# First feed-forward of a decoder layer: from one pass over three token chunks to chunk 0 alone and then chunks 1 and 2 together

## Chip, cores and metric

The kernel runs on one core of a Trainium2 chip. The metric is the device time of one execution in microseconds (us); the kernel before took 2404.62 us, the median of three runs (2401.56 to 2405.68).

## What is computed

One decoder layer for 1024 prompt tokens and 8 sample tokens (1032 tokens of 1024 features): a half-step SwiGLU feed-forward, a mixer (sparse attention and retention), and a second half-step feed-forward, each with a residual and a layer norm. The change touches the first feed-forward and its layer norm.

```python
def swiglu(x, wg, wu, wd):
    return (jax.nn.silu(x @ wg) * (x @ wu)) @ wd

h = layer_norm(ALPHA * x + 0.5 * swiglu(x, ffn1_wg, ffn1_wu, ffn1_wd), ln1_g, ln1_b)
h = h @ w_in                        # split into the mixer's projections
...
h = layer_norm(ALPHA * h + 0.5 * swiglu(h, ffn2_wg, ffn2_wu, ffn2_wd), ln3_g, ln3_b)
```

`wg` and `wu` are 1024 x 2816, `wd` is 2816 x 1024, all float32.

## The kernel before

**Layout.** Activations lie transposed: features on the 128 partitions, tokens along the free axis, in three chunks of `CW` = 344 tokens (0, 1, 2), 8 blocks of 128 features each. A float32 product is made of three TensorE (PE) matmuls on rounded parts (`mm3`): high weight by high activation, high by low, low by high, at lines 169, 170 and 171. High parts are casts on ScalarE (ACT), low parts are differences on VectorE (DVE): `w_split` for weight tiles (L152, L154), L762 and L763 for the tokens. One dense tile of 128 output features for one chunk (`dense`) is thus 24 matmuls of 128x344.

**First feed-forward (class `Ffn`, tag `f1`).** The 2816 inner features are 22 tiles. Each has a gate tile `g`, an up tile `u` and a down tile `d` of 512 KB, loaded once on SyncE's (SP's) DMA queue (`w_raw`, L142) and used for all three chunks (`gateup_chunk`, `down`). The down products (L233 to L235) run by groups of two or four feature tiles and add into the residual `z` (L241).

**Start (`load_x`, `trunk`).** Nine blocks of up to 128 tokens are loaded (`xn`, L741), transposed on PE (`xt`, L754, two groups of four) and cast into the operands `xh` and `xl`. The first weights are split behind the first token blocks, and `z` is summed up on GpSimd (POOL, L768). `bias_rows` makes a table for the attention: a tiny matmul `bt` (L1278), a copy into the scratch tile `bra` in slot 20 (L1280), and a DMA that writes it 128 times over into DRAM (`scr`, L1281). That DMA is issued when all tokens and three feature tiles have been loaded.

**End.** After the last group's downs of a chunk its layer norm runs (`layer_norm`): `pm` (L645), a subtraction and squares on DVE and ACT, `pv` (L667), `pr` (L672), then the operands `h1h` and `h1l` (L682) of the next projections, `pw_ki` first. The norm of chunk 0 runs while PE makes the downs of chunks 1 and 2.

**Second feed-forward (class `Ffn2`, tag `f2`).** It is already split in two passes: `chunk0` makes chunk 0 with plain products, `chunks12` makes chunks 1 and 2 with gate and up by Strassen's seven products of half-size blocks (`ps0` to `ps6`) instead of eight; downs are plain in both. Its weights are loaded twice, by a class `Stream` that loads and splits tiles ahead as slots come free (L338 for whole tiles, L355 and L361 for sums and their split).

**Order.** The program's order on each engine is that in which the code issues; `Sched` interleaves the generators (`load_x`, `bias_rows`, layer norms) by modelled ticks, and on each engine instructions run in that order. Slots `A(g, slot, ...)` are numbered: a tile in a slot waits for whoever still uses the tile before it there.

Of the kernel before, what the change touches and what calls it, by code (L numbers as in the profile page):

```python
# [184 lines left out]
class Ffn:  # L185


    def __init__(self, g, wg, wu, wd, x, z, tag):
        self.g, self.wg, self.wu, self.wd, self.x, self.z, self.tag = g, wg, wu, wd, x, z, tag
        self.gt = {}  # L190
        self.groups = [[0, 1], *[list(range(f, f + 4)) for f in range(2, 22, 4)]]

    def weights(self, ft):
        g = self.g
        return (load_w(g, wcols(self.wg, ft * 128), f"{self.tag}g{ft}"), load_w(g, wcols(self.wu, ft * 128), f"{self.tag}u{ft}"))

    def gate_tile(self, ft):
        s = 14 + 2 * (ft % 5)
        self.gt[ft] = (A(self.g, s, f"gh_{self.tag}{ft}", F32R), A(self.g, s + 1, f"gl_{self.tag}{ft}", F32R))

    def gateup_chunk(self, ft, w, c):
        g, nc = self.g, self.g.nc
        x = self.x[c]
        th, tl = self.gt[ft]
        sl = slice(c * CW, (c + 1) * CW)
        pg = dense(g, w[0], x, f"pg_{self.tag}{ft}_{c}")
        s = g.ms.tile([P, CW], F32, tag="silu", name=f"s_{self.tag}{ft}_{c}", bufs=2)
        nc.scalar.activation(s, pg, AF.Silu)
        g.s.tick(0)
        pu = dense(g, w[1], x, f"pu_{self.tag}{ft}_{c}")  # L210
        nc.vector.tensor_tensor(out=s, in0=s, in1=pu, op=OP.mult)  # L211
        nc.scalar.copy(th[:, sl], s)
        nc.vector.tensor_tensor(out=tl[:, sl], in0=s, in1=th[:, sl].bitcast(F32), op=OP.subtract)
        g.s.tick(0)

    def gateup(self, ft):
        w = self.weights(ft)
        self.gate_tile(ft)
# [3 lines left out]
    def loaddown(self, grp):
        return [load_w(self.g, self.wd[ft * 128:(ft + 1) * 128, :].rearrange("p (k f) -> p k f", k=8), f"{self.tag}d{ft}") for ft in grp]

    def down(self, grp, ws, t0, t1, o):

        g = self.g
        sl = slice(t0, t1)
        p = bank(g, 'mm', f"pd_{self.tag}{grp[0]}_{t0}_{o}")
        for i, ft in enumerate(grp):  # L230
            th, tl = self.gt[ft]
            wh, wl = ws[i]
            g.nc.tensor.matmul(p[:, 0:t1 - t0], wh[:, o, :], th[:, sl], start=i == 0, stop=False)  # L233
            g.nc.tensor.matmul(p[:, 0:t1 - t0], wh[:, o, :], tl[:, sl], start=False, stop=False)  # L234
            g.nc.tensor.matmul(p[:, 0:t1 - t0], wl[:, o, :], th[:, sl], start=False, stop=i == len(grp) - 1)  # L235
        t = t0
        while t < t1:
            c = t // CW
            e = min(t1, (c + 1) * CW)
            z = self.z[c][:, o, t - c * CW:e - c * CW]  # L240
            g.nc.vector.scalar_tensor_tensor(out=z, in0=p[:, t - t0:e - t0], scalar=0.5 / ALPHA, in1=z, op0=OP.mult, op1=OP.add)  # L241
            t = e
        g.s.tick(0.44 * len(grp) * (t1 - t0) / CW)

    def middle(self):

        for gi, grp in enumerate(self.groups):
            for ft in grp:
                if ft not in self.gt:
                    self.gateup(ft)  # L250
            if gi + 1 < len(self.groups):
                if self.groups[gi + 1][0] not in self.gt:
                    self.gateup(self.groups[gi + 1][0])
                ws = self.loaddown(grp)
                for o in range(8):
                    for c in range(NCH):
                        self.down(grp, ws, c * CW, (c + 1) * CW, o)
# [2217 lines left out]
```

## Time and profile before

| what | us |
|---|---|
| median of three runs | 2404.62 |
| the profiled execution | 2399.24 |
| its span on the core | 2397.5 |
| PE busy in the span | 2284.9 (95%) |
| DVE busy | 1490.2 (62%) |
| ACT busy | 943.4 (39%) |
| GpSimd busy | 379.4 (16%) |
| first feed-forward's last matmul starts | 776.0 |

The span is that of the profiled execution, whose own time is 2399.24 us, 5.4 us under the median. PE's busy share is an average: what a stage is limited by is read from the windows and waits of that stage. "DMA share" in a window is the mean busy share of the core's 16 DMA engines.

### The profile page before, as it was taken

What the parts mean: (1) busy time and instruction counts of PE and PEld (TensorE: products, weight loads), DVE (VectorE), ACT (ScalarE), POOL (GpSimd) and SP (SyncE); (2) the same over time, 40 slices, a digit from 0 to 9 for tenths busy, and PEclk for the clock granted to TensorE, in tenths of its full rate; (3) what the DMA queues carried; (4) which work ended last, traced back from release to release, by engine and by line L of the source; (5) the groups of instructions that cost most, each with busy time, mean ns of one, the idle gap of its engine ahead of it and who ended that gap; (6) DMA issues with size and microseconds to landing.
All of it is one profiled execution on the core that took longest, in us unless ns stands there. A gap on an engine that the chain in (4) does not pass through costs nothing.

```text
span 2397.5 us, 36677 instructions
## 1 busy us (share of the span) xinstructions
PE 2284.9 (95%) x14495; PEld 2206.5 (92%) x14495; DVE 1490.2 (62%) x3262; ACT 943.4 (39%) x1722; POOL 379.4 (16%) x375
## 2 busy tenths in 40 slices
PE   8999999999999999898988999999999899999996
PEld 7999999999999998787767988899999899999995
DVE  5322323232226678678977667869756788787876
ACT  3121211212023555877445666436433443343331
POOL 3000000000003313454024225541000200000002
PEclk9999999999999999999989999989999999999998
DMA  6121211111021211222221215553544322222311
GB/s 160 36 79 36 62 45 53 40 49 53 18 71 58 88 33 46 56 75 56 66 72 33 55 46 180 178 161 99 157 132 138 117 77 71 88 72 65 94 54 48
DMA packets 211522, 186.93 MB, mean 78 GB/s; under 512 B 12074, under 2 KB 195190, under 8 KB 210582
## 3 DMA queue, kind: packets, MB, share of 16 engines
q1 hardware_dynamic: 206998, 171.93, 24.0%
q0 software_dynamic: 4352, 12.65, 1.9%
q8 instruction: 114, 1.87, 0.3%
q14 instruction: 58, 0.48, 0.1%
HBM read 163.39 MB, written 21.17 MB: 77 GB/s over the span
## 4 chain that ended last, share of the span: by engine, by line
PE 79%; DVE 10%; ACT 6%; issue 3%; DMA 1%; POOL 1%; POOLq 0%; SPq 0%; ACTq 0%; DVEq 0%
PE pu_f L169 5%; PE pg_f L171 5%; PE pu_f L171 5%; PE pu_f L170 5%; PE pg_f L169 4%; PE pg_f L170 4%; PE pd_f L233 3%; PE pd_f L235 3%; PE pd_f L234 3%; PE pds_f L467 2%; PE pds_f L468 2%; PE pds_f L469 2%; ACT ja L1019 2%; PE ps_f2U L169 2%; PE ps_f2U L170 2%
## 5 line engine op out<-in xcount | busy, mean ns | idle before, releaser
L211 DVE TENSOR_TENSOR s_f<-s_f,pu_f 128x344 f32<-128x344 f32 x66 | 33.8, 512 | 233.0 <-PE pu_f L171 233.0
L171 PE MATMUL pg_f<-xh,wl_f1g 128*128 128x344 f32 x528 | 169.6, 321 | 1.1 <-DVE wl_f1g L154 1.1
L169 PE MATMUL pg_f<-xh,wh_f1g 128*128 128x344 f32 x528 | 169.8, 322 | 0.0
L170 PE MATMUL pg_f<-xl,wh_f1g 128*128 128x344 f32 x528 | 169.1, 320 | 0.5 <-DVE xl L763 0.5
L233 PE MATMUL pd_f<-gh_f,wh_f1d 128*128 128x344 f32 x528 | 169.5, 321 | 0.0
L235 PE MATMUL pd_f<-gh_f,wl_f1d 128*128 128x344 f32 x528 | 169.2, 320 | 0.0
L169 PE MATMUL pu_f<-xh,wh_f1u 128*128 128x344 f32 x528 | 168.8, 320 | 0.0
L234 PE MATMUL pd_f<-gl_f,wh_f1d 128*128 128x344 f32 x528 | 168.8, 320 | 0.0
L170 PE MATMUL pu_f<-xl,wh_f1u 128*128 128x344 f32 x528 | 168.6, 319 | 0.0
L171 PE MATMUL pu_f<-xh,wl_f1u 128*128 128x344 f32 x528 | 168.5, 319 | 0.0
L241 DVE SCALAR_TENSOR_TENSOR z<-pd_f,z 128x344 f32<-128x344 f32 x144 | 73.9, 516 | 142.7 <-PE pd_f L235 142.5
L471 DVE SCALAR_TENSOR_TENSOR z<-pds_f,z 128x344 f32<-128x344 f32 x160 | 82.4, 516 | 73.3 <-PE pds_f L469 73.3
L606 POOL TENSOR_TENSOR lns_l<-z 128x344 f32<-128x344 f32 x4 | 5.4, 1348 | 711.1 <-DVE z L241 694.8
L716 POOL TENSOR_TENSOR yt<-yt,lot 128x512 f32<-128x512 f32 (+1 forms) x7 | 7.2, 1041 | 693.8 <-DVE lot L709 692.1
L467 PE MATMUL pds_f<-gs_f,wh_f2ds 128*128 128x344 f32 x352 | 113.0, 321 | 0.0
L468 PE MATMUL pds_f<-gs_f,wh_f2ds 128*128 128x344 f32 x352 | 112.7, 320 | 0.0
L469 PE MATMUL pds_f<-gs_f,wl_f2ds 128*128 128x344 f32 x352 | 112.5, 320 | 0.0
L1019 ACT ACTIVATE ja<-key,zt 128x1024 bf16<-128x1024 int16 (+5 forms) x90 | 93.8, 1043 | 42.9 <-DVE zt L1030 35.1
L152 ACT CAST wh_f1g<-wr_f1g 128x1024 fp32r<-128x1024 f32 x22 | 23.1, 1049 | 221.0 <-PE pd_f L234 170.4
L171 PEld LDWEIGHTS pg_f<-xh,wl_f1g 128*128 128x128 f32 x528 | 99.8, 189 | 1.4 <-DVE wl_f1g L154 1.4
L170 PEld LDWEIGHTS pg_f<-xl,wh_f1g 128*128 128x128 f32 x528 | 99.8, 189 | 0.8 <-DVE xl L763 0.8
L169 PEld LDWEIGHTS pg_f<-xh,wh_f1g 128*128 128x128 f32 x528 | 99.8, 189 | 0.2
(718 smaller groups left out, 7602.1 us busy)
## 6 DMA issues: line engine op xcount, KB each, us to landing
wr_f1g<-in_ffn_wg_dram SPq DMA_DIRECT2D x22, 512.0 KB
wr_f1u<-in_ffn_wu_dram SPq DMA_DIRECT2D x22, 512.0 KB
wr_f1d<-in_ffn_wd_dram SPq DMA_DIRECT2D x22, 512.0 KB
wr_f2u<-in_ffn_wu_dram SPq DMA_DIRECT2D x22, 512.0 KB
wr_f2g<-in_ffn_wg_dram SPq DMA_DIRECT2D x22, 512.0 KB
wr_f2dp<-in_ffn_wd_dram SPq DMA_DIRECT2D x22, 512.0 KB
wr_f2G<-in_ffn_wg_dram SPq DMA_DIRECT2D x22, 512.0 KB
wr_f2U<-in_ffn_wu_dram SPq DMA_DIRECT2D x22, 512.0 KB
```

Source lines behind the costliest of these rows:

```text
L169: g.nc.tensor.matmul(ps, w[0][:, k, :], x[0][:, k, :], start=first and i == 0, stop=False)
L170: g.nc.tensor.matmul(ps, w[0][:, k, :], x[1][:, k, :], start=False, stop=False)
L171: g.nc.tensor.matmul(ps, w[1][:, k, :], x[0][:, k, :], start=False, stop=last and i == n - 1)
L233: g.nc.tensor.matmul(p[:, 0:t1 - t0], wh[:, o, :], th[:, sl], start=i == 0, stop=False)
L234: g.nc.tensor.matmul(p[:, 0:t1 - t0], wh[:, o, :], tl[:, sl], start=False, stop=False)
L235: g.nc.tensor.matmul(p[:, 0:t1 - t0], wl[:, o, :], th[:, sl], start=False, stop=i == len(grp) - 1)
L241: g.nc.vector.scalar_tensor_tensor(out=z, in0=p[:, t - t0:e - t0], scalar=0.5 / ALPHA, in1=z, op0=OP.mult, op1=OP.add)
L467: g.nc.tensor.matmul(ps, wh[:, o, :], th, start=i == 0, stop=False)
L468: g.nc.tensor.matmul(ps, wh[:, o, :], tl, start=False, stop=False)
L469: g.nc.tensor.matmul(ps, wl[:, o, :], th, start=False, stop=i == len(grp) - 1)
L471: g.nc.vector.scalar_tensor_tensor(out=z, in0=ps, scalar=0.5 / ALPHA, in1=z, op0=OP.mult, op1=OP.add)
L1019: nc.scalar.activation(jk[:, 0:n], key[b], AF.Sign, bias=t[:, j:j + 1], scale=-1.0, accum_out=cnt[:, j:j + 1])
```

## The change

The first feed-forward is now made by `Ffn2` as well, and the class `Ffn` goes. Its first pass makes chunk 0 with plain products, and each finished block of `z[0]` is written to DRAM (`parked`). The second pass makes chunks 1 and 2 with the seven products for gate and up; the slots of chunk 0 hold the operands that this needs (`T1` to `T4`, by `load_x` and `lefts`). `z[0]` is then read back (`z10p`), and the layer norm of chunk 0 runs during the last downs of chunks 1 and 2 (`last`). All 66 weight tiles are loaded twice. `load_x` brings the tokens in at a slower pace, and copies `z` on ACT (L733 after). The number of PE matmuls of 128x344 in the first feed-forward goes from 4752 to 4488: each of the 11 pairs of feature tiles takes, for gate and again for up, 7 products of 12 matmuls in place of 8.

```diff
-class Ffn:
...
-            for c in range(NCH):
-                self.gateup_chunk(ft, w, c)
...
+    def end(self):
+        for p in (9, 10):
+            self.drop('s', self.pairs[p])
+            self.g.fs.put(*self.gt.pop(p)[1])
...
+def lefts(g, B, a, b, slots, free):
...
+    V.tensor_tensor(out=d3, in0=b[:, 4:8, :], in1=b[:, 0:4, :], op=OP.subtract)
+    V.tensor_tensor(out=d2, in0=d3, in1=a[:, 0:4, :], op=OP.add)
+    yield 1.0
+    split4(g, B, 'T2', slots[0], d2)
+    yield 2.0
+    split4(g, B, 'T3', slots[1], d3)
+    V.tensor_tensor(out=d2, in0=a[:, 4:8, :], in1=d2, op=OP.subtract)
+    while not free():
+        yield 0.25
+    split4(g, B, 'T4', slots[2], d2)
...
 def load_x(g, xp, xs, x, B, z):
...
+                nc.scalar.copy(z[c][:, ks, sl], src)
                 t = e
+        if b + 3 < 9:
+            fetch(b + 3)
         g.s.t += 0.6
-        if b in (2, 5, 8):
-            c = b // 3
-            nc.gpsimd.tensor_tensor(out=z[c], in0=x[c][0].bitcast(F32), in1=x[c][1].bitcast(F32), op=OP.add)
         g.xb = b + 1
-        yield 0 if b < 2 else 2.0
+        yield 0 if b < 2 else 10.0
...
     s.tick(0)
-    r0 = [w_raw(g, wcols(w, 0), n) for w, n in ((f1.wg, "f1g0"), (f1.wu, "f1u0"))]
+    f1.st.nraw = 2
+    f1.st.fetch()
     s.until(lambda: g.xb >= 3)
-    w0 = [tuple(w_split(g, r) for r in r0)]
+    f1.st.ahead(2)
...
     br = s.add(bias_rows(g, i['rel_bias'], i['oh'], g.scr), 6.0)
...
+        while s.live(br):
+            yield 1.0
+        g.fs.put(20, 21)
...
+    def parked(o):
+        psum['ls'].add(o)
+        nc.sync.dma_start(zscr[0][:, o * CW:(o + 1) * CW], z[0][:, o, :])
...
+    f1.chunk0(x[0], hook, parked)
+    psum['out'] = True
+    setbanks(g, ch=[0, 1, 2, 3], dn=[4, 5], aux=[6, 7])
+    f1.chunks12(B, ready)
...
+    z[0] = X8(g, "z0", "z10p")
+    for q in range(2):
+        nc.sync.dma_start(z[0][:, 4 * q:4 * q + 4, :].rearrange("p k t -> p (k t)"), zscr[0][:, 4 * q * CW:(4 * q + 4) * CW])
...
+    lns[0] = s.add(ln1(0, psum['ls']), 4.0)
...
+    for c in (1, 2):
         ls = LnSum(g, z[c], f"l1{c}")
...
+        f1.last(c, after)
...
         lns[c] = s.add(ln1(c, ls))
+    f1.end()
```

**The start, on ACT.** The first casts of the program, before and after. `xt0_0` to `xt2_1` are the transposed token blocks 0 to 2, whose casts the first product of chunk 0 needs; `wr_f1g0` is the loaded gate tile 0, `wh_` its high part.

Before:

```order
L762 CAST xh0_91<-xt0_0_112 128x4x128
L762 CAST xh0_91<-xt0_1_119 128x4x128
L762 CAST xh0_91<-xt1_0_128 128x4x128
L762 CAST xh0_91<-xt1_1_135 128x4x128
L152 CAST wh_f1g0_163<-wr_f1g0_106 128x1024
L762 CAST xh0_91<-xt2_0_144 128x4x88
L762 CAST xh0_91<-xt2_1_153 128x4x88
```

After:

```order
L273 CAST wh_f1g0_169<-wr_f1g0_0_105 128x1024
L731 CAST xh0_91<-xt0_0_109 128x4x128
L731 CAST xh0_91<-xt0_1_117 128x4x128
L273 CAST wh_f1u0_175<-wr_f1u0_0_107 128x1024
L273 CAST wh_f1g1_206<-wr_f1g1_0_173 128x1024
L733 COPY z10_95<-xt0_0_109 128x4x128
L733 COPY z10_95<-xt0_1_117 128x4x128
L273 CAST wh_f1u1_238<-wr_f1u1_0_179 128x1024
L731 CAST xh0_91<-xt1_0_127 128x4x128
L731 CAST xh0_91<-xt1_1_135 128x4x128
```

Four weight casts and the copies of `z` now stand between the casts of the token blocks.

**The store of the table, on SP's queue.** `scr` is the table's write, `wr_f1g3`, `wr_f1u4`, `wr_f1dp2` are weight tiles, `xn7` a token block.

Before:

```order
L142 DMA wr_f1d0_808<-in_ffn1_wd_dram 128x1024
L142 DMA wr_f1d1_814<-in_ffn1_wd_dram 128x1024
L1281 DMA scr_60<-bra_253 1024x1x384
L142 DMA wr_f1g3_1012<-in_ffn1_wg_dram 128x8x128
L142 DMA wr_f1u3_1018<-in_ffn1_wu_dram 128x8x128
```

After:

```order
L710 DMA xn6_311<-in_x_prompt_dram 128x1024
L1254 DMA scr_60<-bra_256 1024x1x384
L710 DMA xn7_418<-in_x_prompt_dram 128x1024
L228 DMA wr_f1u4_0_424<-in_ffn1_wu_dram 128x8x128
L228 DMA wr_f1dp2_0_461<-in_ffn1_wd_dram 128x1024
L228 DMA wr_f1dp3_0_483<-in_ffn1_wd_dram 128x1024
L228 DMA wr_f1g5_0_505<-in_ffn1_wg_dram 128x8x128
L228 DMA wr_f1u5_0_527<-in_ffn1_wu_dram 128x8x128
```

The store now stands among the loads of the first pass. The tile `wl_f1u3` (low part of up tile 3) is made in slot 20, where `bra` lay, so that its split on DVE waits for the store to have landed; the load `wr_f1u5` in turn waits for the buffer that this split reads. On PE the first user of `wl_f1u3` stands here after:

```order
L171 MATMUL pg_f14_621<-xh0_91,wl_f1g4_502 128x344
L721 MATMUL xt6_0_666<-ident_65,xn6_311 128x128 x4
L721 MATMUL xt6_1_672<-ident_65,xn6_311 128x128 x4
L171 MATMUL pu_f13_585<-xh0_91,wl_f1u3_480 128x344
L169 MATMUL pu_f13_585<-xh0_91,wh_f1u3_479 128x344
```

There are 158 matmuls of 128x344 and three transposed blocks on PE between `bt` and that `pu_f13` matmul. Before, the next tile in slot 20 is `gh_f13`, which is written only after nine products of `gateup_chunk` (48 matmuls each).

**The end, on PE.** `pds_f118_2_4` is the fifth of eight down products of chunk 2, `pv_l11` a step of the layer norm of chunk 1, `pw_ki_0` the first projection, of chunk 0.

Before:

```order
L234 MATMUL pd_f118_688_7_6317<-gl_f121_5687,wh_f1d21_5873 128x344
L235 MATMUL pd_f118_688_7_6317<-gh_f121_5686,wl_f1d21_5875 128x344
L169 MATMUL pw_ki_0_6344<-h1h0_6128,wh_ki_5956 128x344
L170 MATMUL pw_ki_0_6344<-h1l0_6129,wh_ki_5956 128x344
L171 MATMUL pw_ki_0_6344<-h1h0_6128,wl_ki_5958 128x344
```

After:

```order
L405 MATMUL pds_f118_2_4_7270<-gs1_f120_6894,wl_f1ds21_6829 128x344
L635 MATMUL pv_l11_7308<-ones_70,lns_l11_7018 128x1 x3
L169 MATMUL pw_ki_0_7379<-h1h0_7180,wh_ki_7108 128x344
L169 MATMUL pw_qi0_0_7430<-h1h0_7180,wh_qi0_7142 128x344
L169 MATMUL pw_kr0_0_7466<-h1h0_7180,wh_kr0_7462 128x344
L170 MATMUL pw_ki_0_7379<-h1l0_7181,wh_ki_7108 128x344
L171 MATMUL pw_ki_0_7379<-h1h0_7180,wl_ki_7110 128x344
L169 MATMUL pw_ki_0_7379<-h1h0_7180,wh_ki_7108 128x344
L170 MATMUL pw_ki_0_7379<-h1l0_7181,wh_ki_7108 128x344
L403 MATMUL pds_f118_2_5_7291<-gs0_f118_6606,wh_f1ds18_6772 128x344
```

Seven projection matmuls on chunk 0's normalised operands now stand ahead of 36 downs of chunk 2. Between `pm_l10` and `pw_ki_0` there were 168 downs and there are 132; between `pm_l11` and `pv_l11` there were 101 matmuls of 128x344 and there are 36. From `pw_qi0_1` on, PE's order is the same in both.

## Rows read from the trace of the kernel before

**Rows 1.** Page: busy us, share, instructions; costliest group: busy, mean ns, idle before.

```profile
PE 2284.9 (95%) x14495; PEld 2206.5 (92%) x14495; DVE 1490.2 (62%) x3262; ACT 943.4 (39%) x1722; POOL 379.4 (16%) x375
L169 PE MATMUL pg_f<-xh,wh_f1g 128*128 128x344 f32 x528 | 169.8, 322 | 0.0
```

**Rows 2.** 50-us windows: length, busy (count) per engine PE PEld DVE ACT POOL, clock, DMA.

```profile
0.00:50.00 50.00, 41.01 (x239) 36.70 (x240) 32.43 (x38) 21.45 (x38) 19.86 (x9) 1.00 0.64 182
200.00:250.00 50.00, 50.00 (x318) 50.00 (x318) 15.19 (x27) 3.31 (x5) 0.00 (x0) 1.00 0.08 22
1700.00:1750.00 50.00, 50.00 (x320) 49.81 (x319) 30.91 (x41) 16.62 (x22) 0.00 (x0) 1.00 0.47 142
1900.00:1950.00 50.00, 40.73 (x236) 40.20 (x235) 49.37 (x91) 28.21 (x48) 14.70 (x9) 0.90 0.31 102
2000.00:2050.00 50.00, 50.00 (x319) 50.00 (x319) 39.91 (x74) 18.03 (x32) 0.00 (x0) 1.00 0.24 74
```

**Rows 3.** Timeline, PE, 0 to 22 us: start, length, instruction [idle before].

```profile
11.07 0.66 PE L169 MATMUL pg_f<-xh,wh_f1g 128*128 128x344 f32 x1
15.86 0.45 PE L171 MATMUL pg_f<-xh,wl_f1g 128*128 128x344 f32 x1
20.13 1.07 PE L754 MATMUL xt<-ident,xn 128*128 128x128 f32 x8 [1.92 <-issue]
```

**Rows 4.** Timeline, SP's queue, first 130 us.

```profile
11.35 0.32 SPq L1274 DMA_DIRECT2D bra<-in_rel_bias_dram  x1
12.65 0.32 SPq L1275 DMA_DIRECT2D bra<-in_oh_dram  x1
36.38 0.81 SPq L1281 DMA_DIRECT2D scr<-bra  x1
75.69 0.38 SPq L142 DMA_DIRECT2D wr_f1g<-in_ffn_wg_dram  x1
```

**Rows 5.** Costs of single instructions: timeline and line groups, ACT and DVE.

```profile
5.53 0.59 ACT L762 CAST xh<-xt 128x512 fp32r<-128x512 f32 x1 [3.53 <-PE xt L754]
L152 ACT CAST wh_f1g<-wr_f1g 128x1024 fp32r<-128x1024 f32 x22 | 23.1, 1049 | 221.0 <-PE pd_f L234 170.4
L154 DVE TENSOR_TENSOR wl_f1g<-wr_f1g,wh_f1g 128x1024 fp32r<-128x1024 f32 x16 | 19.6, 1226 | 40.1 <-ACT wh_f1g L152 40.1
```

**Rows 6.** DMA issues of the first 130 us: transfer, count, KB each.

```profile
scr<-bra SPq DMA_DIRECT2D x1, 1536.0 KB
```

**Rows 7.** 5-us windows around the end of that transfer, columns as in Rows 2.

```profile
65.00:70.00 5.00, 5.00 (x33) 5.00 (x33) 0.19 (x1) 0.46 (x1) 0.00 (x0) 1.00 0.43 48
70.00:75.00 5.00, 5.00 (x34) 5.00 (x33) 1.40 (x3) 1.89 (x3) 0.00 (x0) 1.00 0.02 5
```

**Rows 8.** Waits of PE, first 130 us: total, times, longest.

```profile
PE pg_f L171 <- DVE wl_f1g L154: 1.1, 1, 1.1
```

**Rows 9.** Waits of PE, 1868 to 1960 us.

```profile
PE ps_f2U L169 <- DVE pc_f2G L533: 5.5, 1, 5.5
PE ps_f2G L169 <- DVE lot L628: 3.8, 1, 3.8
```

**Rows 10.** 10-us window after those waits, columns as in Rows 2.

```profile
1920.00:1930.00 10.00, 10.00 (x52) 10.00 (x53) 9.85 (x16) 7.09 (x11) 0.48 (x1) 0.79 0.43 134
```

**Rows 11.** Timeline, DVE, in the same stretch.

```profile
1896.19 3.68 DVE L705 BATCH_NORM_STATS2 lot<-yp 128x6 f32<-128x512 f32 x6
```

**Rows 12.** Timelines, PE and DVE, first layer norm of chunk 0.

```profile
746.79 0.74 PE L645 MATMUL pm_l<-lns_l,ones 128*128 128x344 f32 x2
757.00 0.80 PE L667 MATMUL pv_l<-ones,lns_l 128*128 128x1 f32 x6
772.27 1.59 DVE L682 TENSOR_TENSOR h1l<-z,h1h 128x1376 fp32r<-128x1376 f32 x1
776.16 0.32 PE L169 MATMUL pw_ki<-h1h,wh_ki 128*128 128x344 f32 x1
```

**Rows 13.** Waits of PE, 700 to 850 us.

```profile
PE pv_l L667 <- DVE lns_l L657: 2.8, 2, 2.0
```

More of the change, by code (lines that the diff above doesn't have):

```diff
@@ L182, in dense @@
     return ps
-class Ffn:
[L188 to L218, printed above, removed]
-        for c in range(NCH):
-            self.gateup_chunk(ft, w, c)
[L222 to L257, printed above, removed]
@@ L264, in __init__, with get, take @@
         self.ids = list(ids)
+        self.first = ()
     def __len__(self):
         return len(self.ids)
-    def get(self):
-        return self.ids.pop(0)
+    def get(self, long=False):
+        q = next((q for q in self.ids if long and q in self.first), self.ids[0])
+        self.ids.remove(q)
+        return q
     def put(self, *ids):
         self.ids += ids
+    def take(self, ids):
+        self.ids = [q for q in self.ids if q not in ids]
 class Stream:
@@ L324, in want, with want_all @@
         return self.made[key]
+    def want_all(self):
+        while self.steps:
+            assert self.step(), "no room"
     def done(self, key):
@@ L504, in gates @@
         g = self.g
-        sl = [g.fs.get() for _ in range(3)]
+        sl = [g.fs.get(True) for _ in range(3)]
         t = [A(g, q, f"gs{j}_{self.tag}{f}", F32R, 3 * CW) for j, q in enumerate(sl)]
@@ L594, in last, with halves_of, split4 @@
             self.down('s', grp, c, {f: tiles[(f, c)] for f in grp}, o, after)
+def halves_of(t):
+    return t[:, 0:4, :], t[:, 4:8, :]
+def split4(g, B, nm, slot, src):
+    B[nm] = halves_of(X8(g, slot, f"op{nm}", F32R))
+    g.nc.scalar.copy(B[nm][0], src)
+    g.nc.vector.tensor_tensor(out=B[nm][1], in0=src, in1=B[nm][0].bitcast(F32), op=OP.subtract)
+def lefts(g, B, a, b, slots, free):
+    V = g.nc.vector
+    d3, d2 = (g.ms.tile([P, 4, CW], F32, tag="lnq", name=f"d{j}", bufs=2) for j in (3, 2))
+    V.tensor_tensor(out=d3, in0=b[:, 4:8, :], in1=b[:, 0:4, :], op=OP.subtract)
[8 more added lines that the diff above has]
+    split4(g, B, 'T4', slots[2], d2)
 class LnSum:
@@ L1988, in ln1, with after @@
         return layer_norm(g, z[c], ls.s, ln['ln1_g'], ln['ln1_b'], out, f"l1{c}", done)
[L1990 to L1999 removed]
+    lns[0] = s.add(ln1(0, psum['ls']), 4.0)
+    f1.st.want_all()
+    own = [q for q in g.fs.ids if q in ok][:6]
+    g.fs.take(own)
+    g.raws, g.ri, g.pairs, g.pi = own[0:2], 0, [tuple(own[2:4]), tuple(own[4:6])], 0
+    g.lo_eng = [nc.vector]
+    for nm in ('ki', 'qi0'):
+        rX[nm] = w_raw(g, wcols(w_in, colX[nm]), nm)
+    for c in (1, 2):
+        ls = LnSum(g, z[c], f"l1{c}")
+        def after(o):
+            ls.add(o)
+            if c == 1 and o in (4, 6):
+                nm = ('ki', 'qi0')[(o - 4) // 2]
                 wX[nm] = w_split(g, rX[nm])
+        f1.last(c, after)
         if c == 1:
@@ L2004, in trunk @@
         lns[c] = s.add(ln1(c, ls))
+    f1.end()
+    s.drain(lns[0])
+    g.fs.put(psum['slot'])
+    more = [q for q in g.fs.ids if q in ok][:6]
+    g.pairs += [tuple(more[j:j + 2]) for j in (0, 2, 4)]
     kst, kl = A(g, 18, "kst", F32R), A(g, 19, "kl", F32R)
```

104 lines of the change are left out of this document (43 added, 61 removed).

## Prediction

> **What bounds the kernel now.** I read the page first: PE is busy 95% of the span, and the costliest groups are the first feed-forward's matmuls, with next to no idle time ahead of them [rows 1]. So the time goes with the number of matmuls, except where PE waits. The 50-us windows say what one matmul costs: 318 to 320 in 50 us at full clock, 0.157 us each (the mean of 322 ns in rows 1 overlaps its neighbours and is not a rate). That holds in the first feed-forward, where DVE is busy 15.2 of 50 us, in the plain first pass of the second, at DVE 30.9 and 142 GB/s, and in its seven-product pass, at DVE 39.9 [rows 2]. So both passes that the first feed-forward is to get already run on this chip with PE full. What is left are the joints: the start, the change from one pass to the next, and the layer norm at the end. The reader should look there for PE below 50 in 50: 41.0 at the start, 40.7 at the joint of the second feed-forward [rows 2].
>
> **Term 1, the products.** 4752 matmuls become 4488: 264 x 0.157 = -41.4 us. Every extra DVE and ACT step of the seven products (+518 and +220 instructions) lies beside full PE, as in rows 2; if that cover were gone, the slower rival below gives the price. Twice the weights is cheap as long as a tile comes in time: in the plain pass three 512 KB tiles serve 72 matmuls, 11.3 us, which is 139 GB/s, what the window of 142 GB/s already shows; the peak needed is below the 182 GB/s of the first window [rows 2].
>
> **Term 2, the start.** Before, the stream begins at 11.07, at 0.29 us a matmul (half clock) until 15.86 [rows 3]. After, ACT casts four weight tiles and copies z between the casts of the token blocks, so it waits in order for loads. Loads land one after another: bra's first part is issued when one landing frees it and its second part at the next, 11.35 and 12.65, so 1.3 us per 512 KB [rows 4]. Gate tile 0 is the fourth load and lands near 8.8, up 0 10.1, gate 1 11.3, up 1 (a token block is ahead of it) 13.9, gate 2 15.2. With 1.05 us per weight cast and 0.59 per token cast or copy [rows 5]: cast of gate 0 to 9.85, two token casts 11.0, up 0 12.1, gate 1 13.1, two copies 14.3, up 1 15.3, two casts 16.5, two copies 17.7, gate 2 18.8, two short casts 19.8, then DVE's low parts: the full stream from about 21.2. About 13 matmuls at half clock cost 1.7 more, six later token blocks 0.8 each but for the last (20.13 to the next matmul [rows 3]), together 4.2, and bt 0.7: PE has lost 27.9 us in all. Before, 164 matmuls of 128x344 have begun by 50 us, a loss of 50 - 164 x 0.157 = 24.3 (the window counts 239 with some 75 transposes and small ones [rows 2]). So +3.6; bounds 0 (the casts find everything landed and PE starts as before) and 7.
>
> **Term 3, the table's store.** Before, it is issued at 36.38, when nothing is left to load until 75.69 [rows 4]. It moves 1536 KB [rows 6] at 48 GB/s with 0.43 of the engines' time, and ends about 70.5: the 65 to 70 window is still at 0.43, the next at 0.02 [rows 7]. That is 34.1 us, which nobody waits for. After, the split of up tile 3 on DVE stands behind it through slot 20. bt comes 83 matmuls and one token block after the stream's start: 21.2 + 13.0 + 1.7 + 0.8 = 36.8, the store is issued at 37.6 and lands at 71.8, the split (1.23 [rows 5]) ends at 73.1. PE gets to the matmul that needs it after bt (0.7), 158 matmuls (24.8) and three token blocks (2.4), at 64.7. It waits 8.4 us, with everything behind it in its order; DVE's next splits (up 4, the downs) and SP's load of up 5 are queued behind the same split, but up 4 is needed 22 matmuls later only. The half clock after a wait like this: a window after one holds 52 matmuls in place of 64 [rows 10], 12 x 0.157 = 1.9. Together +10.3; bounds 0 (the store is quick beside the loads, or goes early enough) and 16.
>
> The store could also begin later than it is issued: four loads of 512 KB stand ahead of it on the queue, and loads land one after another [rows 4], so up to 4 x 1.3 = 5.2 us more if none of them has run. The Trainium skill, page "DMA: Bandwidth & Descriptors", section "Queues, rings and completion order", says that each DMA engine consumes its ring's descriptors in order. By that page the store waits for whatever of the four is still queued, and the time would be up to 2388; the landings in rows 4 agree with such an order, but no row shows a load behind the store.
>
> **Term 4, a wait that goes.** PE's wait for the low part of a gate tile at 115 us, 1.1 us [rows 8], belongs to the old order of loads: -1.3 with the restart.
>
> **Term 5, from pass 1 to pass 2.** The second feed-forward pays 5.5 + 3.8 us there [rows 9] and 1.9 for the clock [rows 10], 11.2 in all, because DVE has the splits for the seven products and the output layer norm at once (49.4 of 50 busy [rows 2], six statistics of 3.68 us being the norm's first part [rows 11]). The first feed-forward has the splits, the downs' sums and T2 to T4 there, but no layer norm on DVE: its sums go to POOL. Counting the instructions from the last group's first down to the third product chain by their durations I get 51.5 us of DVE work beside 54.7 us of PE work. It just fits. I take +1, near the lower end, since the row of 11.2 holds work that is missing here; bounds 0 and 11.2.
>
> **Term 6, the end.** Before, from pm of chunk 0 to its operands (h1l done at 773.9) takes 27.1 us, and from pm to pv 10.2 us [rows 12]; 168 downs cover the first, 26.4 us, and PE waits 2.8 in all [rows 13]. After, 132 downs (20.7 us) are left ahead of the first projection, and 36 matmuls (5.7 us) between pm and pv of chunk 1, in place of 101. PE would wait 10.2 - 5.7 = 4.5 for pv, some 2 more for the operands (27.1 - 20.7 - 4.5), and 2 to 3 for pr of chunk 1 and the norm of chunk 2, which now follow close on each other: about 9, against 2.8. I take +6; bounds 0 and 10. The reload of z[0] (1.4 MB, by the 1.3 us per 512 KB of rows 4 under 4 us) lies under 96 downs of chunk 1 (15 us) and costs nothing; without that cover it would cost its 4 us once.
>
> The sums that POOL no longer makes and the slower pace of the token blocks lie beside full PE: nothing. From the second projection group of chunk 1 on PE's order is unchanged, so nothing more is to come.
>
> **Sum.** -41.4 + 3.6 + 10.3 - 1.3 + 1 + 6 = -21.8 us. From the profiled execution, 2399.2 us (span 2397.5 and 1.7 around it), that gives 2377.4. The median of the runs shown is 5.4 higher; the comparison is with it, so **2383 us**.
>
> **Rivals.** (A) The store costs nothing: 2383 - 10 = 2373. For it: the stall rests on one slot and on a margin of 8 us in 65, and the store may run faster when it starts in a stretch with other traffic. Against it: its 34 us were measured with the queue free. (B) The joint between the passes costs what it costs in the second feed-forward: 2383 + 10 = 2393. For it: the code is the same class and 51.5 against 54.7 leaves little, with waits inside that chain not counted. Against it: without the norm. (C) Slower: the stream of weights in pass 1 does not run ahead. Each of 66 tiles takes 1.3 + 1.05 + 1.23 = 3.6 us from the queue's turn to the split, and one tile lasts PE 3.8 us; as slots are also held by token blocks and the table until some 100 us in, tiles could come late by a part of this. From 0.4 us a tile on, 26 us, the gain is gone; at 0.6, 40 us, the time is 2423. Against it: the same pass in the second feed-forward has PE at 50.00 [rows 2]. (D) The change does not do what it says, the number of matmuls staying: excluded by the order, which has 264 fewer of 128x344, and none elsewhere changed.
>
> **Chances.** Forecast, 2377 to 2389: 0.53. A: 0.17. B, or the store's later start (at most 2388): 0.18. Both and a worse end, 2398 to 2409: 0.08. C: 0.04, D: 0. The range for 8 in 10 goes from 2367 (A with a better start) to 2398 (B with the end's upper bound). A measurement here can tell about 0.2%, 4.8 us: faster means under 2399.8 and gets 0.88, the same 0.08, slower 0.04.
>
> **What will show it.** The number of 128x344 matmuls and 50.00 of 50 in the windows from 100 to 400 and in the pass after (term 1, C). The first full product near 21 us on PE (term 2). One wait of PE on the low part of up tile 3 near 65 us, about 8 us long, that ends 1.2 us after the table's store has landed (term 3, A). PE's waits between 270 and 310 us, where the passes meet, on sums or splits of DVE: 0 to 2 us, or 9 (term 5, B). PE's waits on pv, h1h, h1l and pr before the mixer, 9 in all (term 6). The forecast is wrong above all if PE has gaps spread over pass 1, or if the joints do not stand where I put them.

## The result, and the profile after

The changed kernel takes **2379.3 us** (median of five runs, 2376.15 to 2386.46); the kernel before, run beside it, 2401.6. The ratio is 0.9914 with a 95% interval of 0.9889 to 0.9940, so 22 us less. The forecast was 2383; of the 4 us between them 3 are the kernel before itself, which took 2404.6 when the forecast was made and 2401.6 in this run. The profiled execution went from 2399.24 to 2376.15 us, 23.1 less; the sum ahead of the result had 21.8.

The page and the 50-us windows of the changed kernel, columns as in [rows 1] and [rows 2]:

```profile
PE 2245.4 (95%) x14231; PEld 2165.0 (91%) x14231; DVE 1773.3 (75%) x3780; ACT 1077.2 (45%) x1942; POOL 361.8 (15%) x372
```

```profile
0.00:50.00 50.00, 35.34 (x200) 32.83 (x201) 21.41 (x32) 27.58 (x45) 0.69 (x6) 1.00 0.70 202
50.00:100.00 50.00, 41.97 (x258) 41.51 (x257) 25.61 (x38) 18.76 (x30) 0.00 (x0) 0.90 0.72 186
100.00:150.00 50.00, 50.00 (x323) 49.62 (x322) 34.96 (x46) 20.91 (x30) 0.00 (x0) 1.00 0.48 142
200.00:250.00 50.00, 50.00 (x319) 49.72 (x318) 29.53 (x43) 15.57 (x21) 0.00 (x0) 1.00 0.47 142
300.00:350.00 50.00, 49.52 (x314) 48.98 (x313) 44.28 (x82) 19.66 (x36) 0.00 (x0) 1.00 0.31 91
400.00:450.00 50.00, 50.00 (x319) 49.91 (x318) 41.42 (x78) 18.91 (x34) 0.00 (x0) 1.00 0.25 75
750.00:800.00 50.00, 49.08 (x298) 47.49 (x298) 38.65 (x61) 27.35 (x47) 15.04 (x12) 0.95 0.32 118
```

PE is busy 39.5 us less and DVE 283 us more, still beside it. From 100 to 300 and from 350 to 700 us PE is full, 318 to 323 matmuls in 50 us, as in [rows 2]; the plain pass moves 142 GB/s, the pass with the seven products has DVE at 38 to 44. What is not full is the start, the stretch from 50 to 100 and the end of the feed-forward near 750. The timeline of PE at the start and at the table's store, that of SP's queue for the store, and that of DVE:

```profile
4.57 1.94 PE L721 MATMUL xt<-ident,xn 128*128 128x128 f32 x8 [4.57 <-DMA xn<-in_x_prompt_dram]
13.42 1.97 PE L721 MATMUL xt<-ident,xn 128*128 128x128 f32 x8 [6.91 <-ACT z L733]
18.57 1.97 PE L721 MATMUL xt<-ident,xn 128*128 128x128 f32 x8 [3.18 <-ACT z L733]
20.47 0.66 PE L169 MATMUL pg_f<-xh,wh_f1g 128*128 128x344 f32 x1
...
21.81 0.66 PE L170 MATMUL pg_f<-xl,wh_f1g 128*128 128x344 f32 x1
...
24.27 0.32 PE L169 MATMUL pg_f<-xh,wh_f1g 128*128 128x344 f32 x1
```

```profile
37.85 0.81 SPq L1254 DMA_DIRECT2D scr<-bra  x1
46.34 2.82 SPq L710 DMA_DIRECT2D xn<-in_x_prompt_dram  x1
49.25 4.40 SPq L228 DMA_DIRECT2D wr_f1u<-in_ffn_wu_dram  x1
```

```profile
72.17 1.23 DVE L274 TENSOR_TENSOR wl_f1u<-wr_f1u,wh_f1u 128x1024 fp32r<-128x1024 f32 x1 [5.35 <-DMA scr<-bra]
```

```profile
64.39 1.03 PE L721 MATMUL xt<-ident,xn 128*128 128x128 f32 x8
73.45 0.65 PE L171 MATMUL pu_f<-xh,wl_f1u 128*128 128x344 f32 x1 [8.03 <-DVE wl_f1u L274]
```

The second and third token block now wait for copies of z on ACT (6.9 and 3.2 us; before, [rows 3], the first product began at 11.07). DVE's split of up tile 3 waits for the store's landing at 72.2, and PE for that split for 8.03 us. After the wait PE runs at half clock until 78.98: the window has 22 matmuls in 5 us, where 32 fit, at a granted clock of 0.61:

```profile
75.00:80.00 5.00, 5.00 (x22) 5.00 (x22) 2.69 (x3) 3.49 (x4) 0.00 (x0) 0.61 0.89 274
```

The joint of the two passes and the end, as waits of PE, with the timeline at the end:

```profile
PE ps_f1U L169 <- DVE pc_f1G L469: 0.5, 1, 0.5
```

```profile
PE pv_l L635 <- DVE lns_l L625: 2.9, 2, 2.5
PE pkt L1113 <- DVE zt L905: 2.0, 1, 2.0
PE pw_ki L170 <- DVE h1l L650: 0.4, 1, 0.4
```

```profile
721.98 0.74 PE L613 MATMUL pm_l<-l10s,ones 128*128 128x344 f32 x2
...
735.83 0.72 PE L635 MATMUL pv_l<-ones,l10s 128*128 128x1 f32 x6
...
738.39 0.74 PE L613 MATMUL pm_l<-lns_l,ones 128*128 128x344 f32 x2
...
748.35 1.41 PE L635 MATMUL pv_l<-ones,lns_l 128*128 128x1 f32 x6 [2.54 <-DVE lns_l L625]
749.62 0.63 PE L169 MATMUL pw_ki<-h1h,wh_ki 128*128 128x344 f32 x1
```

```profile
750.00:755.00 5.00, 4.62 (x17) 4.18 (x17) 4.70 (x6) 2.13 (x4) 3.07 (x2) 0.53 0.69 285
```

The joint costs 0.5 us of waits; that of the second feed-forward, in [rows 9], costs 9.3. At the end PE waits 2.5 us for `pv` of chunk 1 and then runs at half clock (granted 0.53): 17 matmuls in 5 us, where 32 fit.

**A point to measure by.** The last matmul of the first projection, `pw_ki` of chunk 2, comes after all that the change touches and has the same work ahead of it in every kernel but e4. In the views of that tile (times of the first and the last start), before and after:

```profile
L171 PE MATMUL pw_ki<-h1h,wl_ki x24: 316/320/322, 776.5 to 825.7; 128*128 128x344 f32 x24
```

```profile
L171 PE MATMUL pw_ki<-h1h,wl_ki x24: 314/318/488, 751.7 to 803.4; 128*128 128x344 f32 x24
```

825.7 to 803.4: -22.3 us. "The point" below is this one, and the experiments are read by it as well as by their times. The two traces of the changed kernel agree on it within half a microsecond (803.0 in a0), but on the way they differ by more: chunk 0's first norm step `pm` starts at 721.98 in the one and at 720.4 in the other. So a difference of 2 us between two single traces shows little.

### The profile page after: what moved, and what is told of

It is laid out like the page before. It is cut to its first block, busy times and chain, and to the rows that moved or that the text cites. A ratio compares the mean times of both kernels' runs of the same rounds, so it can differ in the third digit from the quotient of the medians.

```text
span 2374.4 us, 37113 instructions
## 1 busy us (share of the span) xinstructions
PE 2245.4 (95%) x14231; PEld 2165.0 (91%) x14231; DVE 1773.3 (75%) x3780; ACT 1077.2 (45%) x1942; POOL 361.8 (15%) x372
## 3 DMA queue, kind: packets, MB, share of 16 engines
q1 hardware_dynamic: 234838, 209.36, 29.4%
## 4 chain that ended last, share of the span: by engine, by line
PE 77%; DVE 10%; ACT 5%; DMA 3%; issue 2%; POOL 1%; SPq 0%; POOLq 0%; ACTq 0%; DVEq 0%
PE pds_f L403 5%; PE pds_f L404 4%; PE pds_f L405 4%; PE pdp_f L403 2%; PE pu_f L171 2%; PE pdp_f L404 2%; PE pu_f L169 2%; PE pdp_f L405 2%; PE pu_f L170 2%; PE ps_f2U L169 2%; PE ps_f2U L170 2%; PE ps_f2U L171 2%; PE pg_f L169 2%; PE ps_f1U L169 2%; PE pg_f L170 2%
## 5 line engine op out<-in xcount | busy, mean ns | idle before, releaser
L407 DVE SCALAR_TENSOR_TENSOR z<-pds_f,z 128x344 f32<-128x344 f32 x320 | 164.7, 516 | 134.1 <-PE pds_f L405 133.1
L407 DVE SCALAR_TENSOR_TENSOR z<-pdp_f,z 128x344 f32<-128x344 f32 x160 | 80.4, 513 | 47.6 <-PE pdp_f L405 47.4
L403 PE MATMUL pds_f<-gs_f,wh_f1ds 128*128 128x344 f32 x352 | 114.2, 325 | 0.1
L404 PE MATMUL pds_f<-gs_f,wh_f1ds 128*128 128x344 f32 x352 | 113.0, 321 | 0.0
L405 PE MATMUL pds_f<-gs_f,wl_f1ds 128*128 128x344 f32 x352 | 112.9, 321 | 0.0
L1458 DVE TENSOR_TENSOR p<-pT,p 128x512 fp32r<-128x512 f32 (+2 forms) x112 | 55.0, 497 | 26.6 <-ACT p L1457 23.5
L403 PEld LDWEIGHTS pds_f<-gs_f,wh_f1ds 128*128 128x128 f32 x352 | 66.6, 189 | 1.4 <-DVE z L407 0.3
L404 PEld LDWEIGHTS pds_f<-gs_f,wh_f1ds 128*128 128x128 f32 x352 | 66.6, 189 | 0.2
L403 PEld LDWEIGHTS pds_f<-gs_f,wh_f2ds 128*128 128x128 f32 x352 | 66.4, 189 | 0.2 <-ACT gs_f L465 0.2
L405 PEld LDWEIGHTS pds_f<-gs_f,wl_f1ds 128*128 128x128 f32 x352 | 66.5, 189 | 0.0
L404 PEld LDWEIGHTS pds_f<-gs_f,wh_f2ds 128*128 128x128 f32 x352 | 66.3, 188 | 0.0
L405 PEld LDWEIGHTS pds_f<-gs_f,wl_f2ds 128*128 128x128 f32 x352 | 66.3, 188 | 0.0
L171 PE MATMUL pu_f<-xh,wl_f1u 128*128 128x344 f32 x176 | 57.4, 326 | 8.0 <-DVE wl_f1u L274 8.0
```

The costliest lines, as they stand in the source:

```text
L171: g.nc.tensor.matmul(ps, w[1][:, k, :], x[0][:, k, :], start=False, stop=last and i == n - 1)
L403: g.nc.tensor.matmul(ps, wh[:, o, :], th, start=i == 0, stop=False)
L404: g.nc.tensor.matmul(ps, wh[:, o, :], tl, start=False, stop=False)
L405: g.nc.tensor.matmul(ps, wl[:, o, :], th, start=False, stop=i == len(grp) - 1)
L407: g.nc.vector.scalar_tensor_tensor(out=z, in0=ps, scalar=0.5 / ALPHA, in1=z, op0=OP.mult, op1=OP.add)
L1458: nc.vector.tensor_tensor(out=pl[:, js, ts], in0=ptv[:, js, ts], in1=ph[:, js, ts].bitcast(F32), op=OP.subtract)
```

## The experiments

| run | this | before, beside it | ratio, 95% interval | the point |
|---|---|---|---|---|
| changed kernel | 2379.3 | 2401.6 | 0.9914 (0.9889 to 0.9940) | 803.4 |
| again (a0) | 2382.3 | 2406.5 | 0.9915 (0.9887 to 0.9942) | 803.0 |
| e1, slot kept | 2386.2 | 2408.9 | 0.9912 (0.9888 to 0.9936) | 805.0 |
| e2, store by head | 2407.0 | 2408.9 | 0.9990 (0.9974 to 1.0006) | 826.5 |
| e3, start | 2379.3 | 2408.9 | 0.9873 (0.9848 to 0.9898) | 798.5 |
| e4, eighth product | 2425.0 | 2408.9 | 1.0063 (1.0044 to 1.0082) | 847.1 |
| e5, store on GpSimd's queue | 2399.2 | 2399.5 | 0.9998 (0.9976 to 1.0020) | 824.9 |
| e6, store on ACT's queue | 2388.9 | 2399.5 | 0.9955 (0.9934 to 0.9975) | 812.7 |
| e7, load at the joint | 2383.9 | 2399.5 | 0.9922 (0.9900 to 0.9945) | 807.8 |
| e8, norm later | 2384.4 | 2399.5 | 0.9933 (0.9910 to 0.9956) | 807.0 |
| e9, store from DRAM | 2368.6 | 2406.5 | 0.9855 (0.9822 to 0.9887) | 793.6 |
| e10, e3 and e9 | 2362.8 | 2406.5 | 0.9822 (0.9787 to 0.9856) | 785.7 |
| e11, e10, reload earlier | 2364.6 | 2406.5 | 0.9839 (0.9806 to 0.9873) | 787.7 |

Theory at the outset: the sum of the prediction, term by term. The rival for each term stands in its expectation.

### e4: is it the products?

```diff
             mm3(g, ps, w, B[b], range(4))
+            if i == 6 and self.tag == 'f1':
+                mm3(g, ps, w, B[b], range(4))
             self.st.done((key, a))
```

> The last of the seven products of every chain of the first feed-forward is made twice, the second over the first: 264 matmuls of 128x344 more, as many as the change took away, and nothing else. Theory of term 1: PE sets the time in the whole second pass, so the time goes up by 264 x 0.157 = 41.4 us: 2421. Rival: the second pass is in part set by DVE (41 of 50 us busy) or the loads, and some of the extra products find room: less than +35, under 2414.

The point goes from 803.4 to 847.1: +43.7. Waits at the end grow by 1.8 of these (`pw_ki` 1.5 in place of 0.4, 0.7 on a down); 41.9 are left for 264 matmuls, 0.159 each. The joint's 0.5 us wait is gone. So PE sets the time in the whole second pass, and the products saved are worth what term 1 says.

### e1: what holds up tile 3, the slot or what is behind the store?

```diff
-        g.fs.put(20, 21)
+        g.fs.put(21)
...
         s.drain(ld)
+        g.fs.put(20)
```

> Only the slot is changed: the table's tile bra keeps slot 20 until the first pass's last group, so that no weight tile of the first pass waits for the store of the table; the store itself stays where it is on the queue. Theory slot: the split of up tile 3 was held by the slot alone, PE's 8.0 us wait near 65 us goes, and with it 1.9 us of half clock: 2379.3 - 10 = about 2369. Theory queue order: the loads issued behind the store finish only after it, so the next tile, up 4, comes at about 75 and PE, which is there near 69, waits 6 to 8 us for it instead: about 2378, within 2 us of the changed kernel. I expect the second.

The wait on `wl_f1u` at 73.45 is gone, and the point is 1.6 us later, not 10 earlier. PE's timeline of e1 in that stretch:

```profile
67.55 1.03 PE L721 MATMUL xt<-ident,xn 128*128 128x128 f32 x8
73.47 1.94 PE L721 MATMUL xt<-ident,xn 128*128 128x128 f32 x8 [4.88 <-DMA xn<-in_x_prompt_dram]
76.20 0.65 PE L169 MATMUL pu_f<-xh,wh_f1u 128*128 128x344 f32 x1 [0.79 <-ACT wh_f1u L273]
...
77.46 0.65 PE L171 MATMUL pu_f<-xh,wl_f1u 128*128 128x344 f32 x1 [0.32 <-DVE wl_f1u L274]
```

The 1.6 us later are within what two traces of one kernel differ by; 10 us earlier would not be. PE gets 3 us further (68.6 in place of 65.4) and then waits 4.9 us for a token block and 1.1 for up tile 4, both loaded behind the store, and all at half clock in between. The slot was one hold of two; with it gone the other takes its place. Whether that is the order on SP's queue or the engines' time, e5 and e6 were to tell.

### e5 and e6: the store on another queue

```diff
-    nc.sync.dma_start(scr, row.unsqueeze(1).broadcast_to((8, 128, 384)))
+    nc.gpsimd.dma_start(scr, row.unsqueeze(1).broadcast_to((8, 128, 384)))
```

(e6: `nc.scalar`; both with e1's edit.)

> As e1 (the table's tile keeps its slot through the first pass), and the store of the table is issued from GpSimd's queue in place of SP's; same bytes, same place in the program. Theory queue order: loads on SP's queue are no longer behind the store on the engines, arrive 1.3 us apart again, and PE's wait near 65 us goes: 2379 - 10 = about 2369 where the changed kernel takes 2379. Rival: what counts is the engines' time, of which the store takes about half for 34 us whatever its queue; then tiles still come late and 4 us or more of the wait stay.

> As e5, with ACT's queue in place of GpSimd's. Both theories as there: about 2369 if only the order on SP's queue held the loads back, 2373 or more if the store's share of the engines does.

Both are slower than the changed kernel, by 21.5 and 9.3 us at the point; the theory that only the order on SP's queue held the loads back falls. The loads on SP's queue now are issued without delay (up tile 4 at 38.95 and 39.37 us) and still don't arrive. The waits of ACT and then of PE, of e5 and of e6:

```profile
ACT wh_f1u L273 <- DMA wr_f1u<-in_ffn_wu_dram: 29.4, 1, 29.4
```

```profile
PE pdp_f L403 <- DVE z L407: 28.6, 1, 28.6
```

```profile
ACT wh_f1u L273 <- DMA wr_f1u<-in_ffn_wu_dram: 19.1, 1, 19.1
```

```profile
PE pdp_f L403 <- DVE z L407: 17.0, 1, 17.0
```

ACT stands at the cast of up tile 4 for 29.4 and 19.1 us until its load has landed, and behind it in ACT's order are the casts that the down products need; PE's wait is put down to DVE, which had long been waiting for ACT. So while the store runs, a load that shares its engines lasts almost as long as the store, on whichever queue either is. The Trainium skill says so in part: page "DMA: Bandwidth & Descriptors", section "Issuing engines are not separate DMA queues", has transfers of all issuing engines interleave on the same 16 DMA engines; by that another queue saves nothing, and e5 and e6 agree. It doesn't give the loads' part of those engines; the DMA packets of the traces show it. Up tile 4 is 1024 packets of 512 bytes. In the changed kernel 512 of them pass from 54.4 to 56.7 us, while the store runs, and the other 512 only from 72.7 on, behind the store's last packet (71.8). In e6 the second half passes from 53.8 to 71.1, one packet of the load to one of the store; what held it until 53.8 is not shown. The two queues in 10 us of e6 (57 to 67) and of e5 (60 to 70), the store's first: packets, MB, share of the 16 engines.

```profile
q10 hardware_dynamic: 312, 0.48, 44.0%
q1 hardware_dynamic: 312, 0.16, 5.3%
```

```profile
q0 software_dynamic: 105, 0.48, 48.4%
q1 hardware_dynamic: 106, 0.05, 1.8%
```

As many packets of the load as of the store pass, but one of the load (512 bytes) takes 0.03 us and one of the store 0.22 in e6 (1536 bytes) and 0.74 in e5 (4608 bytes). So the order on SP's queue does hold half of a load back, and another queue puts in its place a turn for turn that leaves the load 5 or 2% of the engines' time; with the longer packets of e5 fewer turns come.

### e2 and e9: what makes the store slow?

```diff
-    nc.sync.dma_start(scr, row.unsqueeze(1).broadcast_to((8, 128, 384)))
+    for h in range(8):
+        nc.sync.dma_start(scr[h:h + 1], row[h:h + 1].unsqueeze(1).broadcast_to((1, 128, 384)))
```

> Only the store of the table is changed: eight DMAs, one for each of the eight heads (128 copies of one row of 384 numbers), issued together at the same place, in place of one DMA for all; same bytes, same slot. Theory engines: the one DMA used 8 of the 16 engines because its outer size was 8; with an outer size of 128 all 16 work, the store takes about 17 us in place of 34 and has landed near 55, before PE comes to up tile 3 at 65: the 8.0 us wait goes, about 2369. Rival: the rate of 48 GB/s is that of reading one row over and over, whatever the number of engines; then the store ends near 72 as before, the wait stays 8 us, and the time 2379.

The rival, and worse: PE waits 31.2 us, as the store's last packet passes at 94.7 in place of 71.8. A 5-us window of e2 during the store, beside one of the changed kernel (columns as in [rows 2]):

```profile
75.00:80.00 5.00, 0.00 (x0) 0.00 (x0) 0.00 (x0) 0.00 (x0) 0.00 (x0) 0.50 0.92 28
```

```profile
65.00:70.00 5.00, 0.42 (x4) 0.19 (x2) 0.69 (x1) 1.69 (x4) 0.00 (x0) 0.86 0.45 49
```

Twice as many engines are busy (0.92 against 0.45), and they move 28 GB/s in place of 49. The Trainium skill, page "DMA: Bandwidth & Descriptors", section "Why a DMA increments its semaphore by 16 and not by 1", has the number of engines, at most 16, follow from the outer size, 8 or 128 here; the busy shares agree. But more engines on a single partition's row are slower than 8 on eight, so it is not their number that sets the rate. What is left is the reading of the same few partitions over and over. Hence e9:

```diff
-    nc.sync.dma_start(scr, row.unsqueeze(1).broadcast_to((8, 128, 384)))
+    nc.sync.dma_start(g.scr8, row)
+    yield 2.0
+    nc.sync.dma_start(scr.rearrange("h p f -> p h f"), g.scr8.unsqueeze(0).broadcast_to((128, 8, 384)))
...
+    g.scr8 = dp.tile([8, 384], F32, name="scr8")
```

> Only the store of the table is changed: the eight rows (12 KB) go once to a small buffer in DRAM, and the 128-fold copy is a DMA from that buffer to the table, DRAM to DRAM, with 128 as its outer size. Slot, place on the queue and bytes of the table stay. Theory: the store is slow because its engines read the same few rows of on-chip memory over and over (48 GB/s from eight partitions in the changed kernel, 28 GB/s from one in e2), and while it runs those engines hold up the loads, whatever queue either is on (e5, e6). From DRAM it takes some 5 to 10 us, the tiles behind it come in time, PE's 8 us wait and the half clock after it go: 10 us less than the changed kernel beside it. Rival: the copying of one source 128 times is slow from DRAM too; then the wait stays.

The point is at 793.6, 9.8 and 9.4 us earlier than in the two traces of the changed kernel; the medians, e9 and a0 beside each other, are 13.7 apart, their two profiled executions 10.1. PE has no wait between 25 and 250 us. SP's queue and 2.5-us windows of e9 (store issued at 40.48):

```profile
40.48 0.68 SPq L1256 DMA_DIRECT2D scr<-scr  x1
```

```profile
42.50:45.00 2.50, 2.50 (x16) 2.25 (x16) 1.26 (x2) 1.92 (x5) 0.00 (x0) 1.00 1.02 342
...
52.50:55.00 2.50, 2.50 (x18) 2.50 (x17) 2.12 (x4) 0.21 (x1) 0.00 (x0) 1.00 1.15 323
55.00:57.50 2.50, 2.50 (x18) 2.50 (x18) 1.03 (x2) 0.44 (x1) 0.00 (x0) 1.00 0.43 105
```

From 42.5 to 55 the engines are full at 264 to 374 GB/s, loads included, and at 55 they are back at the pass's level: the store that took 34 us is done in at most 15, with loads running beside it. Its packets of 1536 bytes pass in 6.7 us (43.0 to 49.7; 65 ns each, 224 ns in the changed kernel). e9 takes away both holds at once, as slot 20 is also free as soon as the eight rows have been written; that the slot alone isn't enough, e1 shows. It also writes the table in another order (128 copies outside, 8 heads inside), which was not tried by itself.

### e3: the start

```diff
-    nat, own = {}, [g.fs.get() for _ in range(3)]
+    nat, own, late = {}, [g.fs.get() for _ in range(3)], []
...
-                nc.scalar.copy(z[c][:, ks, sl], src)
+                if b < 3:
+                    late.append((z[c][:, ks, sl], src))
+                else:
+                    nc.scalar.copy(z[c][:, ks, sl], src)
                 t = e
+        if b == 2:
+            for zz, src in late:
+                nc.scalar.copy(zz, src)
...
-    setbanks(g, mm=[0, 1, 2, 3], dn=[4, 5], aux=[6, 7])
+    setbanks(g, aux=[2, 3, 4, 5, 6, 7])
...
     s.until(lambda: g.xb >= 3)
+    setbanks(g, mm=[0, 1, 2, 3], dn=[4, 5], aux=[6, 7])
```

> Only the start is changed: the first three token blocks are transposed into six PSUM banks in place of two, and their copies into z on ACT come after all their casts. Theory of the start: the changed kernel's stream begins at 20.5 instead of 11.1 because on ACT weight casts that wait for loads and copies of z stand between the casts of the tokens; with gate tile 0's cast (to 9.6) and six token casts behind each other the stream begins near 13.5, 7 us earlier, and all that follows is 7 us earlier too, the store of the table and the 8 us wait for it included: about 2372. Rival: PE begins earlier and then waits for the weight tiles up 0 and gate 1, whose casts now come later: less than 3 us gained, 2376 to 2380.

All three token blocks now pass PE at once, and the stream begins at 13.78:

```profile
4.66 5.05 PE L721 MATMUL xt<-ident,xn 128*128 128x128 f32 x24 [4.66 <-DMA xn<-in_x_prompt_dram]
11.99 0.42 PE L169 MATMUL pg_f<-xh,wh_f1g 128*128 128x344 f32 x1 [2.28 <-ACT xh L731]
13.78 0.66 PE L170 MATMUL pg_f<-xl,wh_f1g 128*128 128x344 f32 x1 [1.36 <-DVE xl L732]
```

The point is 4.9 us earlier, between the two theories, and the ratio 0.9873 against 0.9914. The wait on up tile 3 grew from 8.0 to 8.9 us. With the store out of the way (e10 against e9) the same edit is worth 793.6 - 785.7 = 7.9: the start's 7 us were there, and with the late tile 3 of them went again. PE comes to that tile 6 us earlier, but it goes on only when the store has landed, and DVE's split behind the store began at 66.95 in place of 72.17, 5.2 us earlier: that is the gain.

### e7: is the joint cheap because a norm is missing?

```diff
+        s.add(extra(), 4.0)
+
+    def extra():
+        e = z[1][:, 7, :]
+        for _ in range(26):
+            nc.vector.tensor_tensor(out=e, in0=e, in1=e, op=OP.max)
+            yield 0.5
```

> 26 operations of 128x344 on DVE (each z = max(z, z) on one block of the residual, 0.5 us, which changes nothing) are spread over the stretch in which the first pass ends and the seven products begin, about the 13 us that the output layer norm puts there in the second feed-forward. Theory of term 5: DVE has 51.5 us of work there beside 54.7 us of PE, 3 us of room; the rest, 8 to 10 us, appears as waits of PE on DVE near 290 to 320 us, and the time goes up by 8 to 12: about 2389. Rival: the missing norm is not why this joint is cheap, and DVE has room for most of it: up by less than 4.

```profile
L1960 DVE TENSOR_TENSOR z<-z 128x344 f32<-128x344 f32 x25 | 14.5, 581 | 0.2
```

```profile
PE ps_f1G L170 <- DVE opT L546: 1.4, 1, 1.4
PE pdp_f L403 <- DVE z L407: 0.8, 2, 0.4
PE ps_f1U L169 <- DVE pc_f1G L469: 0.4, 2, 0.2
```

14.5 us of DVE work (25 of the 26 lie in this window) cost 2.6 us of waits in place of 0.5, and the point is 4.4 later; counted in matmuls, about 4 of these are lost between 270 and 350 us (475 of 128x344 begin there in place of 501). The edit also moved chunk 0's `pm` on PE, from 722 to 318 us, some 0.6 us of them. Between the theories: the joint had some 10 us of room, not 3. As much DVE work as this does not make the joint as dear as that of the second feed-forward; what else does there is not shown.

### e8: the end

```diff
-    lns[0] = s.add(ln1(0, psum['ls']), 4.0)
+    lns[0] = s.add(ln1(0, psum['ls']), 10.0)
```

> Only the place of the first norm's second and later steps moves: the layer norm of chunk 0 is issued 6 units later, which puts 24 downs of chunk 2 more ahead of the first projection on PE and 16 more ahead of the norm step pv of chunk 1. Theory of cover: PE's waits there (2.9 us on pv, 0.4 on h1l, and some 2.5 us at half clock after them) come from too few downs left to cover the norm; they shrink to 1 us or less and the time goes down by 3 to 5, to about 2375. Rival: the norm itself moves back as much as the cover grows, and the waits only move: within 2 us of the changed kernel.

Nearer to the rival, though outside its 2 us: the point is 3.6 us later. The wait on `pv` is gone, and PE waits 1.6 for `h1h`, 1.1 for a sum and 3.7 for a weight split instead; the norm itself moved back with its cover.

### e10 and e11: together

e10 has the diffs of e3 and e9. e11 adds:

```diff
-    z[0] = X8(g, "z0", "z10p")
+    z[0] = X8(g, "hl2", "z10p")
```

> e3 and e9 together: the earlier start and the store from DRAM. If the two are separate terms of the sum they add: 5 us (the start in e3's trace) and 10 us, so 15 less than the changed kernel beside it. If the earlier start only makes PE come sooner to a tile that is late anyway, about 10 less.

> e10, and the parked chunk 0 is read back into the buffer of T1, which is free three products before that of T4. Theory: DVE waited 1.5 us for the reload before it could begin the norm of chunk 0, whose length sets PE's waits at the end: 1 to 2 us less than e10. Rival: PE's own order of pm and pv holds the norm, and nothing changes: within 1 us of e10.

> The changed kernel itself once more, on the chip of e9 to e11, to compare them with it directly: 0.991 of the kernel before, with PE's 8 us wait near 65 us.

e10 is the best of all: 2362.8 us, 0.9822 of the kernel before (0.9787 to 0.9856), 19.5 us less than the changed kernel beside it, and 17.3 less at the point. The two terms add, and more, as the start is worth 7.9 once no tile is late. e11's earlier reload takes away DVE's wait for it (1.4 us in e10) and changes nothing for the better (2 us later at the point, `pw_ki` waiting 1.5 in place of 0.4 us, a difference that the changed kernel's own two traces show as well).

## Why the prediction was right

Term by term, with what the traces and runs gave:

| term | forecast | measured |
|---|---|---|
| 1 products | -41.4 | -41.9 (e4) |
| 2 start | +3.6 | stream from 21.8 (forecast 21.2); PE at the late tile at 65.4 (64.7) |
| 3 store of the table | +10.3 | wait 8.03 (8.4), and 2.5 at half clock (1.9); e9 gives +9.4 to +9.8 |
| 4 old wait at 115 | -1.3 | gone: PE 50.00 from 100 to 150 |
| 2 to 4 together | +12.6 | +13.8: by 125 us 544 matmuls of 128x344 have begun, 632 before |
| 5 joint | +1 | +0.5 of waits |
| other losses from 125 us to chunk 0's `pm` | 0 | +2.3: 3776 matmuls in 597.0 us, 3952 in 621.8 before |
| 6 end | +6 | +2.5: from `pm` of chunk 0 to the point 81.4 us, 78.9 before |
| sum | -21.8 | -22.3 at the point, -23.1 over the execution |

With the products at -41.4 the measured rows add up to -22.3; rows 2 to 4 are parts of the one below them. The end is measured between lines shown: `pm` starts at 746.79 before [rows 12] and at 721.98 after, the point is at 825.7 and 803.4, and the same 431 matmuls of 128x344 begin between them in both. The second trace of the changed kernel (a0) gives +12.2 for terms 2 to 4 and +3.7 for the end. Between the point and the end of the program the two traces drift by up to 4 us against each other and end 0.8 us apart; two traces of the changed kernel drift by up to 3.

**Right for the reasons given:** terms 1 to 4. The start went as worked out from ACT's order and the landings 1.3 us apart in [rows 4], with each step within about 1.4 us of the forecast; the store was issued at 37.85 (forecast 37.6) and DVE's split began at 72.17 (71.8). Durations and spacings of before, placed in the new order, gave a wait that did not exist before within half a microsecond. The later start of the store that the prediction allowed for (up to 5.2 us) did not come: its first packet passed 1.45 us after the issue in both traces.

**Luck:** that the whole is within half a microsecond of the sum at the point. The end cost 3.5 us less than forecast, and the stretch before it some 3 us more, of which 2.3 stand in no term; what they are is not shown.

**Right in size, wrong in the account, or the other way round:**

- Term 3 named the slot as the hold, and rival A let the stall rest on it. It was one of two holds that end at the same time; e1 removed it and gained nothing. The other is that half of a load behind the store passes only after it, in the order of the queue (up tile 4); e5 and e6 took that order away, the loads then went turn for turn with the store's packets, and 9 to 22 us were lost. Behind all of these are the 34 us for which the store has its engines, and that comes from where it reads (e2, e9). The prediction took those 34 us from [rows 4] and [rows 7] as they were, which is why the number came out all the same.
- Term 5 had the size and too little room: 51.5 us of DVE beside 54.7 of PE should have left 3 us, and e7 found some 10. A sum over a stretch with chosen ends can miss room, as work at its edges can move out; which work did here is not shown.
- Term 6 was too dear. It had 4.5 us for `pv`, 2 for the operands and 2 to 3 for later steps, 9 in all against 2.8 of waits before. There were 2.5 and 0.4, and some 2.5 more at half clock, which the sum had not put there; the whole end takes 2.5 us longer than before, not 6.

One sentence on the kernel ahead of the prediction is too simple: on each engine instructions stand not strictly in the order of the code, since work that is ready may be put ahead (of e7's 26 operations the first ran at 60.3 us, the others from 284 on); the orders shown there, from which the prediction was made, have that in them.
